# The output projection of a hybrid decoder layer by one level of Strassen's algorithm, with the weight sums made early and kept in DRAM

## The chip, the cores and the metric

One core of one Trainium2 chip. The metric is the time of one execution in device microseconds; lower is better. One execution was also recorded by the profiler, and the line numbers below are those of its kernel.

## The reference

The layer maps x of shape (1, 1024, 1024) to the same shape. Cut to what matters here:

```python
h = rmsnorm(x, g_pre) * (1 + scale) + shift        # scale, shift, gate from silu(c) @ w_mod
proj = h @ w_in                                    # split among three groups of heads
y_m = mlstm(...) * silu(mz)                        # 384 columns
y_a = sliding_window_attention(...) * silu(az)     # 384 columns
y_s = stickbreak_attention(...) * silu(sz)         # 256 columns
y = concat([y_m, y_a, y_s]) @ w_out                # (1024, 1024) @ (1024, 1024)
out = x + gate * rmsnorm(y, g_post)
```

The change is in the last product. All is float32.

## The kernel before, in words

Every large matmul is done in three passes: each float32 operand is split into a rounded high part and the low rest (`split`, L68 to L71: ScalarE or another engine casts, VectorE or GpSimd (POOL) subtracts), and TensorE adds high x high, high x low and low x high into one PSUM bank. `hh` and `hl` are the two parts of the transposed activations, eight k-tiles of 128 rows by 1024 tokens. They hold h for the projections, and later y for the output projection. All loads and stores go through `load` (L64) on SyncE's (SP's) queue, in order; a DMA that must wait holds back those behind it.

TensorE's order is written out by hand. Up to the first projections the order of the other engines is too; from there on a scheduler orders VectorE, ScalarE, POOL and SP, and each of them works strictly in the order that it chose.

The stages that the change and the steps below touch:

- The short convolution (L506 to L514) reads `mup`, the mLSTM's input, three slabs of 1027 columns, and makes `cu`; ScalarE's sigmoid of it is `cusg`. Meanwhile TensorE runs the projection `ptmif` (L385), whose banks ScalarE empties (v and igf, L446, L447).
- The gate chain (L562 to L618) computes the mLSTM's gates, max-stabilised running sums of 32 rows. It goes back and forth between TensorE (transposes into `gtr`) and VectorE and ScalarE (fx, ab, b_, a_, cm, mp, M_, em). Between its steps TensorE does pieces of other projections, given by a `Filler` (`fill`), so that it need not wait. Beside it the gate row is summed from `w_gate` (L529 to L540).
- The mLSTM loop (L640 to L749) runs over eight chunks of 128 tokens. Each loads `mbc` (a stabiliser, from DRAM), makes the decay matrix `e` (VectorE subtracts, POOL masks, ScalarE takes the exponential), and multiplies: qps, kps, sps, cps, nps on TensorE, with copies of qps (`q`, L674) on ScalarE and the masked scores `am` on VectorE between them.
- The gated projections: `gated` (L468 to L485) multiplies a branch's output with silu of its z. For y tiles 0 to 5 it splits the result and stores both parts in `d_yh`, `d_yl`; tiles 6 and 7 (from `ys`) are split into `hh`, `hl` near the end (`late`).
- The output projection (L1068 to L1138). `wo_load` loads and splits all of w_out into `woh` and `wol`, and `y_load(n)` brings half n of the tokens (512 columns) of y back into `hh`, `hl`. `out_mm(i, n, k)` does three matmuls for token block i (128 tokens), output half n (512 columns) and k-tile k. The first four blocks fill all eight PSUM banks, k outermost; the last four go one by one. `out_fin(i)` takes the sum of squares on ScalarE straight from PSUM, multiplies by the gate row `gbc`, raises the mean square to the power -1/2 on POOL, and adds x, loaded into `xr` (two buffers).

## Time and profile before

| what | value |
|---|---|
| three runs | 552.19, 553.53, 555.82 us; median 553.53 |
| the profiled execution | 553.0 us |
| its span, first to last instruction | 551.2 us |
| TensorE busy | 523.9 us in 2953 matmuls |
| mean granted TensorE clock | 0.997 of full speed |
| bytes moved by DMA | 96.57 MB |

The profile's rows name an engine (PE is TensorE, DVE VectorE, ACT ScalarE, POOL GpSimd, SPq SyncE's queue), a line, an operation and its tiles as out<-in. In a row of the order of time the first number is the start and the second the duration, both in microseconds; the bracket tells how long the engine had been idle before and what released it. A row by groups ends with busy time and the mean of one in ns. A row of a stretch has its limits and length, then busy time and count of PE, PE's weight loads, DVE, ACT and POOL, then granted clock, DMA share and GB/s. A DMA row ends with the median time from issue to landing. TensorE's matmuls overlap, so their pace is read from starts and counts, not from the duration of one.

### The profile page before, as it was taken

The page shows a single profiled execution, that of the slowest core. Times are in us where ns is not written, and L with a number is a line of the kernel's source. Part 1 is how long each engine was busy: PE and PEld are TensorE (multiplying, and loading weights), DVE is VectorE, ACT ScalarE, POOL GpSimd, SP SyncE. Part 2 cuts the span into 40 slices and gives each one's busy share as a digit, 9 for nine tenths or more (in the row PEclk, how much of TensorE's full clock was granted, in tenths as well). Part 3 has the DMA queues.
Part 4 walks back from the last instruction along what each step waited for, and adds up shares of the span by engine and source line. Part 5 has one row for each costly group of instructions (what it writes and reads, how often), then busy time and mean ns, then how long its engine had stood idle before and what let it go on. Part 6 is the DMA issues. An engine that isn't in the chain of part 4 may idle for free.

```text
span 551.2 us, 8550 instructions
## 1 busy us (share of the span) xinstructions
PE 523.9 (95%) x2953; PEld 449.0 (81%) x2953; DVE 332.5 (60%) x750; ACT 250.3 (45%) x571; POOL 220.6 (40%) x206
## 2 busy tenths in 40 slices
PE   4799999999998999999998999899999999999995
PEld 3577899899987989888786888788888888888884
DVE  4686692053707887678887479787878442108232
ACT  5643533451113333267677568667668432213100
POOL 2365765420033343234534348574766433111000
PEclk9999999999999999999999999999999999999998
DMA  8982360247986455699843389455421169607421
GB/s 307 417 293 75 120 227 21 59 145 219 284 240 222 135 162 125 162 268 299 238 150 98 125 226 249 142 149 167 134 77 59 39 193 404 238 5 238 144 84 69
DMA packets 63659, 96.57 MB, mean 175 GB/s; under 512 B 17600, under 2 KB 36992, under 8 KB 63488
## 3 DMA queue, kind: packets, MB, share of 16 engines
q1 hardware_dynamic: 63616, 96.03, 54.8%
q8 instruction: 23, 0.38, 0.3%
q14 instruction: 20, 0.16, 0.1%
HBM read 69.24 MB, written 25.20 MB: 171 GB/s over the span
## 4 chain that ended last, share of the span: by engine, by line
PE 78%; DVE 10%; DMA 4%; ACT 3%; issue 2%; POOL 2%; SPq 1%; DVEq 0%; POOLq 0%; ACTq 0%
PE pd L359 24%; PE ptav L385 6%; PE mu L233 6%; PE op L1109 5%; PE op L1108 5%; PE op L1107 5%; PE tp L994 3%; DMA ka<-d_akl 3%; PE ptmif L385 2%; DVE cu L509 2%; PE ops L1012 2%; PE ops L1013 2%; PE xps L166 2%; PE z L963 2%; PE mr L197 1%
## 5 line engine op out<-in xcount | busy, mean ns | idle before, releaser
L359 PE MATMUL pd<-hh,wl_d 128*128 128x512 f32 x256 | 71.1, 399 | 0.0
L359 PE MATMUL pd<-hh,wh_d 128*128 128x512 f32 x256 | 70.6, 400 | 0.0
L359 PE MATMUL pd<-hl,wh_d 128*128 128x512 f32 x256 | 70.6, 398 | 0.0
L302 POOL TENSOR_TENSOR wl_d<-w_d,wh_d 128x512 fp32r<-128x512 f32 x32 | 44.0, 1398 | 29.1 <-ACT wh_d L300 19.6
L359 PEld LDWEIGHTS pd<-hh,wh_d 128*128 128x128 f32 x256 | 46.1, 188 | 8.4 <-issue 0.5
L359 PEld LDWEIGHTS pd<-hl,wh_d 128*128 128x128 f32 x256 | 46.1, 188 | 8.0
L359 PEld LDWEIGHTS pd<-hh,wl_d 128*128 128x128 f32 x256 | 45.8, 188 | 7.7
L1108 PE MATMUL op<-woh,hl 128*128 128x512 f32 x128 | 50.6, 396 | 0.0
L1109 PE MATMUL op<-wol,hh 128*128 128x512 f32 x128 | 50.6, 396 | 0.0
L1107 PE MATMUL op<-woh,hh 128*128 128x512 f32 x128 | 50.6, 396 | 0.0
L982 POOL TENSOR_TENSOR sg<-sg,pr 128x512 f32<-128x512 f32 (+1 forms) x30 | 31.1, 1041 | 20.8 <-DVE pr L980 20.6
L857 POOL TENSOR_SCALAR zb<-zb,mx 128x256 f32<-128x256 f32 (+1 forms) x24 | 21.6, 914 | 42.5 <-DVE mx L854 28.4
L70 ACT CAST ah<-tp 128x512 fp32r<-128x512 f32 (+2 forms) x56 | 24.3, 436 | 29.2 <-PE tp L994 20.8
L71 DVE TENSOR_TENSOR al<-tp,ah 128x512 fp32r<-128x512 f32 (+2 forms) x56 | 27.4, 493 | 16.7 <-ACT ah L70 16.0
L1120 ACT ACTIVATE sj<-op 128x512 f32<-128x512 f32 x16 | 9.5, 597 | 50.4 <-PE op L1109 47.9
L1109 PEld LDWEIGHTS op<-wol,hh 128*128 128x128 f32 x128 | 24.0, 188 | 5.9
L1108 PEld LDWEIGHTS op<-woh,hl 128*128 128x128 f32 x128 | 24.0, 188 | 5.8
L1107 PEld LDWEIGHTS op<-woh,hh 128*128 128x128 f32 x128 | 24.0, 188 | 5.8
L1124 POOL TENSOR_TENSOR st<-st,mhalf 128x1 f32<-128x1 f32 x8 | 4.4, 554 | 57.5 <-DVE st L1123 57.5
L847 ACT ACTIVATE zb<-zb,mx 128x256 f32<-128x256 f32 (+1 forms) x48 | 23.2, 488 | 7.8 <-PE az L823 6.6
L980 DVE TENSOR_TENSOR_SCAN pr<-z,mzero 128x128 f32<-128x128 f32 (+3 forms) x32 | 25.6, 815 | 0.6 <-ACT z L971 0.2
L969 ACT ACTIVATE sg<-z 128x512 f32<-128x512 f32 (+3 forms) x48 | 23.8, 496 | 1.3 <-PE z L966 1.1
(247 smaller groups left out, 1328.4 us busy)
## 6 DMA issues: line engine op xcount, KB each, us to landing
wm<-in_w_ss_dram SPq DMA_DIRECT2D x16, 512.0 KB, 7.7
w_d<-in_w_dm_dram SPq DMA_DIRECT2D x16, 512.0 KB, 3.8
xt<-in_x_dram SPq DMA_DIRECT2D x8, 512.0 KB, 7.8
wg<-in_w_gate_dram SPq DMA_DIRECT2D x8, 512.0 KB, 5.8
wo<-in_w_out_dram SPq DMA_DIRECT2D x8, 512.0 KB, 5.2
xr<-in_x_dram SPq DMA_DIRECT2D x8, 512.0 KB, 4.7
out_dram<-ot SPq DMA_DIRECT2D x16, 256.0 KB, 2.3
hh<-d_yh SPq DMA_DIRECT2D x12, 256.0 KB, 6.0
```

The costliest lines, as they stand in the source:

```text
L70: e_hi(dst_h, src)
L71: e_lo.tensor_tensor(out=dst_l, in0=src, in1=dst_h.bitcast(F32), op=ALU.subtract)
L233: T.matmul(mu_acc[j][n], w[:, cs], h[:, k, t], start=(k == 0 and w is wh and h is hh), stop=(k == KT - 1 and h is hl))
L302: G.tensor_tensor(out=wl[:, a:b], in0=z[:, a:b], in1=wh.bitcast(F32)[:, a:b], op=ALU.subtract)
L359: T.matmul(ps, w[:, k, :], h[:, k, t], start=(k == 0 and w is wh and h is hh), stop=(k == KT - 1 and h is hl))
L385: T.matmul(ps[:, 0:self.N], h[:, k, t], w[:, k % 2, :], start=(k == 0 and q == 0), stop=(k == KT - 1 and q == 2))
L969: A.activation(sg[:, 0:w], zps[:, 0:w], AF.Sigmoid)
L980: V.tensor_tensor_scan(out=rev(pr), data0=rev(zps), data1=mzero[:, 0:1].to_broadcast([P, w]), initial=1.0 if nxt is None else nxt, op0=ALU ...
L982: (G if w > 256 and (h > 0 or i > 3) else V).tensor_tensor(out=sg[:, 0:w], in0=sg[:, 0:w], in1=pr[:, 1:w + 1], op=ALU.mult)
L1107: T.matmul(o, hh[:, k, t], woh[:, k, cs], start=(k == 0), stop=False)
L1108: T.matmul(o, hl[:, k, t], woh[:, k, cs], start=False, stop=False)
L1109: T.matmul(o, hh[:, k, t], wol[:, k, cs], start=False, stop=(k == KT - 1))
```

## The change

The 1024 x 1024 x 1024 product is cut into 2 x 2 blocks of 512. Instead of eight block products there are seven, of sums of blocks of y and of w_out (the variant with shared sums S1 to S4 and T1 to T4). With y in rows by token half i and columns by k half r, and w_out in rows by r and columns by output half n:

- P1 = y11 w11, P2 = y12 w21, P6 = S2 T2, P5 = S1 T1, P3 = S4 w22, P7 = S3 T3, P4 = y22 T4, in this order on TensorE. S1 = y21 + y22, S2 = S1 - y11, S4 = y12 - S2, S3 = y11 - y21.
- `w_sums` makes T1 to T4 from w_out, split into two parts, and stores them in DRAM (`d_th`, `d_tl`). For each of four c it loads two 512 KB pieces into the space of `mup`, makes four differences in place, and splits and stores each: 16 differences, 16 casts, 16 low parts, 8 loads and 32 stores of 256 KB. It is called in the gate chain, behind `tcol`.
- `gated` now also stores y unsplit in `d_y`, and for the second half of tokens it no longer splits and stores tiles 0 to 3.
- w11, w21 and w22 are loaded and split in the output stage (`w_ready`, twelve pieces of 256 KB), the T's are loaded there already split (`t_ready`, two loads of 1 MB each, into two pairs of buffers). `y_ready` makes the sums of y into `ysum`, four chunks c each, and splits them into `hh`, `hl` over blocks that are no longer needed.
- Each product has four groups of 12 matmuls, one per token block, into four banks; `e1` to `e7` empty them, adding to what earlier products left in SBUF (`u1`, `u3`, `o11`). Squares are taken from SBUF. `finish` does the rest of `out_fin`, for the first four blocks behind P3 and for the last four behind P4.

```diff
+    def w_sums():
+        for c in range(4):
+            z = mup.rearrange("p a b -> p (a b)")[:, 0:2 * D].rearrange("p (r a b) -> p r a b", r=2, a=2)
+            load(z[:, 0], w_out[c].rearrange("p (a b) -> p a b", a=2))
+            load(z[:, 1], w_out[4 + c].rearrange("p (a b) -> p a b", a=2))
+            w11, w12, w21, w22 = z[:, 0, 0, :], z[:, 0, 1, :], z[:, 1, 0, :], z[:, 1, 1, :]
+            for n, o, a, b in ((0, w11, w12, w11), (2, w12, w22, w12), (1, w22, w22, w11), (3, w21, w22, w21)):
+                V.tensor_tensor(out=o, in0=a, in1=b, op=ALU.subtract)
+                h = gp_.tile([P, 512], F32R, tag="th", bufs=2, name=f"th{c}{n}")
+                l = gp_.tile([P, 512], F32R, tag="tl", bufs=2, name=f"tl{c}{n}")
+                split(h, l, o, A.copy, V)
+                store(d_th[n, :, c, :], h)
+                store(d_tl[n, :, c, :], l)
...
+                store(d_y[dst_j, :, t], y)
+                if n == 1 and dst_j < 4:
+                    return
...
+    w_sums()
     mg_stk.close()
...
+    def y_ready(i, r, chunk):
+        for c in range(4):
+            k = 4 * r + c
+            split(hh[:, k, halves[i]], hl[:, k, halves[i]], chunk(c), A.copy, V)
...
+    w_ready("11", 0, 0)
     fill.through(I_SZ1)
     y_load(0)
+    w_ready("21", 1, 0)
     fill.through(99)
     y_load(1)
+    y_ready(1, 0, lambda c: summed(yc(c), y_quarter(1, 0, c), y_quarter(1, 1, c), ALU.add))
...
+    def product(yi, yr, w, evac):
+        wh, wl = wq_[w]
+        ps = [fbank(f"p{w}_{i}") if i == 3 else ops_.tile([P, 512], F32, tag="op", name=f"p{w}_{i}")
+              for i in range(4)]
+        for i in range(4):
+            t = slice(yi * 512 + i * P, yi * 512 + (i + 1) * P)
+            for c in range(4):
+                k = 4 * yr + c
+                T.matmul(ps[i], hh[:, k, t], wh[:, c, :], start=(c == 0), stop=False)
+                T.matmul(ps[i], hl[:, k, t], wh[:, c, :], start=False, stop=False)
+                T.matmul(ps[i], hh[:, k, t], wl[:, c, :], start=False, stop=(c == 3))
+            evac(i, ps[i])
...
+    def e2(i, ps):
+        V.tensor_tensor(out=o11[i], in0=ps, in1=u1[i], op=ALU.add)
+        square(o11[i], i, 0)
+        V.tensor_tensor(out=o11[i], in0=o11[i], in1=gbc[:, halves[0]], op=ALU.mult)
...
+    def e4(i, ps):
+        V.tensor_tensor(out=u1[i], in0=u1[i], in1=ps, op=ALU.subtract)
+        square(u1[i], 4 + i, 0)
+        finish(4 + i, ((0, u1[i], True), (1, u3[i], False)))
+
+    product(0, 0, "11", e1)
+    t_ready(2)
+    y_ready(0, 0, lambda c: summed(yc(c), yc(c), y_quarter(0, 0, c), ALU.subtract))
+    product(0, 1, "21", e2)
+    t_ready(1)
+    y_ready(0, 1, lambda c: summed(yc(c), y_quarter(0, 1, c), yc(c), ALU.subtract))
+    product(0, 0, "t2", e6)
+    w_ready("22", 1, 1)
...
+    y_ready(0, 0, s3)
+    product(1, 0, "t1", e5)
+    t_ready(3)
+    product(0, 1, "22", e3)
+    t_ready(4)
+    product(0, 0, "t3", e7)
+    product(1, 1, "t4", e4)
```

Since a scheduler sets the order of all engines but TensorE, three places show how their instructions now stand.

VectorE between P2 and P6. Before, the operations on this engine in the output stage were only the finishing of blocks (ot is a block's output, st its statistics):

```order
L71 TENSOR_TENSOR wol_5096<-wo7_5170,woh_5095 128x1024
L1122 TENSOR_TENSOR ot0_5413<-op0_0_5228,gbc_74 128x512
L1123 TENSOR_SCALAR st0_5412<-st0_5412 128x1
L1125 TENSOR_TENSOR ot0_5413<-op0_1_5232,gbc_74 128x512
L1122 TENSOR_TENSOR ot1_5435<-op1_0_5236,gbc_74 128x512
L1128 SCALAR_TENSOR_TENSOR ot0_5413<-ot0_5413,st0_5412,xr0_5410 128x512 x2
```

Now (p21_3 is P2's fourth bank, o113 the sum into which it is emptied; yo and three digits is a loaded chunk of y by i, r and c; ys holds y's tiles 6 and 7):

```order
L1201 TENSOR_TENSOR o113_5369<-p21_3_5454,u13_5361 128x512
L1203 TENSOR_TENSOR o113_5369<-o113_5369,gbc_74 128x512
L1131 TENSOR_TENSOR ysum_5206<-yo102_5339,ys_3612 128x512
L1131 TENSOR_TENSOR ysum_5206<-yo103_5344,ys_3612 128x512
L71 TENSOR_TENSOR hl_102<-ysum_5206,hh_101 128x512
L1131 TENSOR_TENSOR ysum_5206<-ysum_5206,yo000_5431 128x512
...
L1131 TENSOR_TENSOR ysum_5206<-ysum_5206,yo001_5436 128x512
L71 TENSOR_TENSOR hl_102<-ysum_5206,hh_101 128x512 x2
L1131 TENSOR_TENSOR ysum_5206<-ysum_5206,yo002_5441 128x512
L1131 TENSOR_TENSOR ysum_5206<-ysum_5206,yo003_5446 128x512
...
L1131 TENSOR_TENSOR ysum_5206<-yo010_5523,ysum_5206 128x512
```

Where rows are left out stands another low part of a chunk (hl), and one more stands behind the last row. The last two chunks of S1, all of S2 and the first chunk of S4 stand behind the emptying of P2's last bank.

ScalarE at the start of the mLSTM loop (wh_d is a weight cast, sh_aq_1 an eviction, q_0 the copy of qps for chunk 0, e the exponentials of chunks 0 and 1). Before:

```order
L300 CAST wh_d_1688<-w_d_1640 128x1024
L421 ACTIVATE sh_aq_1_1611<-pd_1_1586 128x512
L674 COPY q_0_1622<-qps_1617 96x512
L664 ACTIVATE e_1542<-e_1542 128x512
L664 ACTIVATE e_1634<-e_1634 128x512
L717 COPY num_1672<-nps_1667 128x388
```

Now:

```order
L688 ACTIVATE e_1665<-e_1665 128x512
L688 ACTIVATE e_1757<-e_1757 128x512
L303 CAST wh_d_1811<-w_d_1763 128x1024
L424 ACTIVATE sh_aq_1_1734<-pd_1_1709 128x512
L698 COPY q_0_1745<-qps_1740 96x512
L741 COPY num_1795<-nps_1790 128x388
```

The two exponentials moved ahead of the cast, the eviction and q_0.

VectorE around the start of the gate chain (fx and li are its first operations). Before, they came right behind the convolution:

```order
L509 SCALAR_TENSOR_TENSOR cu_799<-mup_103,col_62,cu_799 128x1024 x9
L587 MEMSET mp_1207 1x36
L569 TENSOR_SCALAR fx_1126<-gtr_1122,bi_1060 32x128
L573 TENSOR_SCALAR li_1125<-gtr_1122,bi_1060 32x128
L574 TENSOR_SCALAR fx_1126<-fx_1126 32x128
```

Now (th and tl are the two parts of a sum, by c and the number of T less one):

```order
L71 TENSOR_TENSOR tl11_1375<-mup_106,th11_1374 128x512
L71 TENSOR_TENSOR tl13_1382<-mup_106,th13_1381 128x512
L558 TENSOR_TENSOR mup_106<-mup_106 128x512
L71 TENSOR_TENSOR tl20_1391<-mup_106,th20_1390 128x512
L592 TENSOR_SCALAR fx_1129<-gtr_1125,bi_1063 32x128
L596 TENSOR_SCALAR li_1128<-gtr_1125,bi_1063 32x128
L597 TENSOR_SCALAR fx_1129<-fx_1129 32x128
L558 TENSOR_TENSOR mup_106<-mup_106 128x512
L425 SCALAR_TENSOR_TENSOR sl_ak0_0_1149<-pd7_0_1076,sh_ak0_0_1148 128x512
L598 TENSOR_TENSOR fx_1129<-fx_1129,ab_1133 32x128
```

The first two rounds of the sums and the first quarter of the third stand ahead of fx, and the rest stands between the operations of the chain.

More of the change, by code (lines that the diff above doesn't have):

```diff
@@ new lines, in rows_of, with square, finish @@
+    def rows_of(name):
+        return [op_.tile([P, 512], F32, tag=name, bufs=4, name=f"{name}{i}") for i in range(4)]
+    u1, u3, o11 = (rows_of(z) for z in ("u1", "u3", "o11"))
+    st = op_.tile([P, NT, 4], F32, name="st")
+    def square(src, i, n):
+        sj = op_.tile([P, 512], F32, tag="sj", bufs=2, name=f"sj{i}_{n}")
+        A.activation(sj, src, AF.Square, accum_out=st[:, i, n:n + 1])
+    def finish(i, parts):
+        xr = op_.tile([P, D], F32, tag="xr", bufs=2, name=f"xr{i}")
+        load(xr, x[i * P:(i + 1) * P, :])
+        s_ = st[:, i, :]
+        V.tensor_scalar(out=s_[:, 2:3], in0=s_[:, 1:2], scalar1=s_[:, 0:1], scalar2=D * EPS, op0=ALU.add, op1=ALU.add)
+        G.tensor_tensor(out=s_[:, 3:4], in0=s_[:, 2:3], in1=mhalf[:, 0:1], op=ALU.pow)
+        for n, o, gate in parts:
+            if gate:
+                V.tensor_tensor(out=o, in0=o, in1=gbc[:, halves[n]], op=ALU.mult)
+        for n, o, _ in parts:
+            V.scalar_tensor_tensor(out=o, in0=o, scalar=s_[:, 3:4], in1=xr[:, halves[n]], op0=ALU.mult, op1=ALU.add)
+            store(out[i * P:(i + 1) * P, halves[n]], o)
@@ new lines, in e7 @@
+    def e7(i, ps):
+        V.tensor_tensor(out=u1[i], in0=ps, in1=u1[i], op=ALU.add)
+        V.tensor_tensor(out=u3[i], in0=ps, in1=u3[i], op=ALU.add)
+        square(u3[i], 4 + i, 1)
+        V.tensor_tensor(out=u3[i], in0=u3[i], in1=gbc[:, halves[1]], op=ALU.mult)
+    def e4(i, ps):
[4 more added lines that the diff above has]
+    t_ready(2)
@@ new lines, in trunk, with s3 @@
+    y_ready(0, 0, lambda c: summed(yc(c), yc(c), y_quarter(0, 0, c), ALU.subtract))
[4 more added lines that the diff above has]
+    w_ready("22", 1, 1)
+    def s3(c):
+        z = y_quarter(0, 0, c)
+        return summed(z, z, y_quarter(1, 0, c), ALU.subtract)
+    y_ready(0, 0, s3)
[4 more added lines that the diff above has]
+    product(0, 0, "t3", e7)
```

93 lines of the change are left out of this document (42 added, 51 removed).

## The prediction

> **What bounds the kernel now.** I read the page's first and fourth parts, then busy time by stretches, then single stretches in order of time.
>
> ```profile
> span 551.2 us, 8550 instructions
> PE 523.9 (95%) x2953; PEld 449.0 (81%) x2953; DVE 332.5 (60%) x750; ACT 250.3 (45%) x571; POOL 220.6 (40%) x206
> PE 78%; DVE 10%; DMA 4%; ACT 3%; issue 2%; POOL 2%; SPq 1%; DVEq 0%; POOLq 0%; ACTq 0%
> ```
>
> TensorE is busy for 95% of the span and is 78% of the chain that ended last, so a microsecond of its work removed is worth a microsecond, unless it waits instead. The stretches show where it has no waits:
>
> ```profile
> 455.20:545.00 89.80, 89.76 (x385) 71.95 (x383) 27.98 (x43) 18.13 (x39) 12.62 (x12) 1.00 0.48 173
> 150.00:170.00 20.00, 17.47 (x90) 14.05 (x89) 6.63 (x11) 3.83 (x6) 7.92 (x7) 1.00 0.80 237
> ```
>
> The output projection is 455.2 to 545.0: 384 matmuls in 89.8 us, 0.2338 us each, with no gap; VectorE is busy for only 28.0 us of it. At 150 to 170, where the mLSTM loop starts, TensorE already idles 2.5 us.
>
> **What is removed.** Seven products of 4 x 4 x 3 = 48 matmuls are 336 instead of 384: 48 x 0.2338 = **-11.2 us**. Nothing else leaves the path.
>
> **What is added in the output stage.** The prices of its operations:
>
> ```profile
> L1120 ACT ACTIVATE sj<-op 128x512 f32<-128x512 f32 x16 | 9.5, 597 | 50.4 <-PE op L1109 47.9 <-DVE st L1123 1.5 <-DVE ot L1128 1.0
> L1122 DVE TENSOR_TENSOR ot<-op,gbc 128x512 f32<-128x512 f32 x8 | 5.5, 691 | 20.4 <-ACT sj L1120 20.1 <-DMA out_dram<-ot 0.2
> L1128 DVE SCALAR_TENSOR_TENSOR ot<-ot,st,xr 128x512 f32<-128x512 f32 x16 | 11.3, 748 | 1.8 <-DMA xr<-in_x_dram 1.2
> L1124 POOL TENSOR_TENSOR st<-st,mhalf 128x1 f32<-128x1 f32 x8 | 4.4, 554 | 57.5 <-DVE st L1123 57.5
> 456.13 1.29 DVE L71 TENSOR_TENSOR hl<-ys,hh 128x512 fp32r<-128x512 f32 x2 [1.83 <-ACT hh L70]
> 459.43 0.62 ACT L70 CAST hh<-ys 128x512 fp32r<-128x512 f32 x1 [2.83 <-POOL ys L484]
> ```
>
> A 128x512 operation takes VectorE 0.69 us, 0.645 in a row of two; a cast takes ScalarE 0.62.
>
> The products follow each other as P1, P2, P6, P5, P3, P7, P4. P1 and P2 need what the old code also had there (y of the first half, unsummed, and w_out), so from 455.2 on P1 ends at 466.4 and P2 at 477.6 (11.2 each). P6 needs the row sum S2 = S1 - y11, four chunks, each a VectorE subtraction, a ScalarE cast and a VectorE subtraction for the low part. VectorE works in order, and in its order two of S1's chunks and all of S2 stand **behind P2's fourth eviction**, although P2 reads none of them. That eviction cannot start before P2's last matmul is done, at 477.8. So: the eviction 0.69, ScalarE's square of it 0.60, the gating multiply that waits for the square 0.68, together 2.0, to 479.8; then to the low part of S2's fourth chunk 13 operations (six sums, six low parts and S4's first sum, which stands between) x 0.645 = 8.4, with the casts beside them, to 488.3; then P6's last two matmuls of its first group, to 488.8. Without the wait this group would end at 477.6 + 2.8 = 480.4. **+8.4 us**: TensorE idles until S2's first chunk at about 483, and then crawls. Bounds: 8.0 if every hand-over is hidden, 10.5 if S2's last two y loads, which are issued behind t1's two loads of 1 MB, land late. These are 2.1 MB from 477.7 on, at the rate of slice 34 of the page's row (404 GB/s) 5.2 us:
>
> ```profile
> GB/s 307 417 293 75 120 227 21 59 145 219 284 240 222 135 162 125 162 268 299 238 150 98 125 226 249 142 149 167 134 77 59 39 193 404 238 5 238 144 84 69
> xr<-in_x_dram SPq DMA_DIRECT2D x8, 512.0 KB, 4.7
> out_dram<-ot SPq DMA_DIRECT2D x16, 256.0 KB, 2.3
> ```
>
> so they end near 483, and the y chunks behind them are there when VectorE comes to them at 485. By the same rate t2 (from 466.5), t3 (from 508.5) and t4 (from about 520 to 528) are in before P6, P7 and P4 (530.8); P5, P3 and P7 find their sums and weights ready, because nothing but P2's evictions stood ahead of them. Their cover is 2 to 6 us; if t4 were later than that, P4 would wait for the difference.
>
> **The end.** Before, it is this:
>
> ```profile
> 544.56 0.40 PE L1109 MATMUL op<-wol,hh 128*128 128x512 f32 x1
> 546.72 1.42 DVE L1128 SCALAR_TENSOR_TENSOR ot<-ot,st,xr 128x512 f32<-128x512 f32 x2
> 547.50 0.99 SPq L64 DMA_DIRECT2D out_dram<-ot  x2
> ```
>
> From the last matmul (544.96) to the end are 6.2 us, 3.1 of them behind the last VectorE operation (548.1). Now each row block is finished in 2.8 us instead of 5.6, and it has two buffers for the x rows: block 7's x load is issued behind block 5's two stores. With P4 ending at 455.2 + 78.4 + 8.4 = 542.0, block 5's stores are issued until about 542.3, x lands 4.7 us later at 547.0, then two operations (1.4) and 3.1: 551.4, 9.4 us behind the last matmul. **+3.2 us**; at least 1.4 (if x were there, VectorE's own chain of subtract, square, gate and two multiplies would end at 546.6), at most 4.
>
> **The start of the mLSTM loop** is not edited, but its ScalarE and POOL order came out another way: q_0's copy now stands behind both decay exponentials, a weight cast and an eviction.
>
> ```profile
> 160.51 0.94 SPq L64 DMA_DIRECT2D mbc<-d_m  x2
> 164.97 1.00 DVE L661 TENSOR_TENSOR e<-tcol,mbc 128x512 f32<-128x512 f32 x1 [7.35 <-DMA mbc<-d_m]
> 161.74 1.05 ACT L300 CAST wh_d<-w_d 128x1024 fp32r<-128x1024 f32 x1 [4.84 <-PE pd L359]
> 163.18 0.57 ACT L674 COPY q<-qps 96x512 f32<-96x512 f32 x1
> 166.62 1.68 POOL L662 TENSOR_SCALAR_AFFINE_SELECT e<-e 128x512 f32<-128x512 f32 x2
> 167.75 1.22 ACT L664 ACTIVATE e<-e 128x512 f32<-128x512 f32 x2 [3.99 <-POOL e L662]
> 163.91 1.06 PE L690 MATMUL sps<-q,cuh 96*128 96x128 f32 x8
> 169.59 1.13 PE L712 MATMUL nps<-v,am 128*128 128x97 f32 x8 [1.00 <-DVE am L692]
> ```
>
> Before, q_0 was there at 163.75 and the exponentials (from 167.75) held up only am. Now mbc is issued ahead of two stores, 1.2 us sooner; e follows 4.5 us behind, at 163.8; the second e ends near 165.7, its mask 166.5, its exponential 167.1, the cast 168.1, the eviction 168.6, q_0 169.1. sps starts at 169.1 instead of 163.9, the old waits behind it vanish, and nps follows after sps, cps and five fillers (2.6 us as before), near 171.7: **+2.0 us** (0 if mbc lands 2 us sooner, +3 if later).
>
> **The sums of w_out** stand in VectorE's and SP's queues ahead of and between the gate chain.
>
> ```profile
> 82.99 1.06 ACT L513 ACTIVATE cusg<-cu 128x1024 f32<-128x1024 f32 x1 [2.74 <-DVE cu L509]
> 87.64 1.06 ACT L513 ACTIVATE cusg<-cu 128x1024 f32<-128x1024 f32 x1 [2.33 <-POOL cu L514]
> 89.18 0.45 PE L385 MATMUL ptmif<-wh_mif,hh 128*128 128x392 f32 x1 [0.93 <-ACT igf L447]
> 107.93 0.34 DVE L569 TENSOR_SCALAR fx<-gtr,bi 32x128 f32<-32x128 f32 x1 [17.86 <-POOL wl_av L302]
> 113.58 0.28 DVE L575 TENSOR_TENSOR fx<-fx,ab 32x128 f32<-32x128 f32 x1 [0.93 <-ACT ab L572]
> 114.65 0.41 DVE L579 TENSOR_TENSOR_SCAN cm<-ones,a__1128 32x128 f32<-32x128 f32 x1
> 116.29 0.12 PE gtr L582
> w_d<-in_w_dm_dram SPq DMA_DIRECT2D x3, 512.0 KB, 3.2
> d_akh<-sh_ak SPq DMA_DIRECT2D x2, 256.0 KB, 2.0
> ```
>
> VectorE idles 17.9 us ahead of fx, and the new work fills that. The convolution has read the first slab of mup at 83.0, so the first half block lands at 86.2, is subtracted by 86.9 and cast by 87.5, just ahead of the third cusg (87.64), behind which TensorE already waits 0.9 us for igf. A round of one c is a load 3.2, then subtraction, cast, low part (1.9), one store (2.4 with its issue) for the two buffers, cast and low part (1.3): about 9 us. Two rounds end near 103 and the first quarter of the third near 106, ahead of fx at 107.9. Between fx and cm stand five more operations, 3.2 us; VectorE waited 0.9 there, cm had 1.2 us to spare before the transpose at 116.29, and ScalarE's table loads come earlier, since a weight cast moved behind them. I take **+0.5 us**, bounds 0 and 6 (below).
>
> **Clock.** Where TensorE idles, the granted clock falls:
>
> ```profile
> 547.00:548.00 1.00, 0.00 (x0) 0.00 (x0) 1.00 (x2) 0.00 (x0) 0.00 (x0) 1.00 0.00 0
> 548.00:549.00 1.00, 0.00 (x0) 0.00 (x0) 0.13 (x1) 0.00 (x0) 0.00 (x0) 0.70 0.65 248
> 549.00:550.00 1.00, 0.00 (x0) 0.00 (x0) 0.00 (x0) 0.00 (x0) 0.00 (x0) 0.50 0.71 277
> ```
>
> 0.70 in one microsecond means half from 548.4 on, 3.4 us behind the last matmul. The two new waits are each about 5 us. The trace never shows it come back. Behind the wait at P6 twelve matmuls crawl at VectorE's pace for 5.6 us, which even half speed (0.47 each) keeps, so the clock may be back by then: **+0.7 us**, bounds 0 and 8.4 (P6's other 36 matmuls all at half speed).
>
> By the Trainium skill, TensorE: Matmul & The Clock Gate, section "HAM oscillation — how this bites in real kernels", gaps beyond about 3.4 us throttle TensorE to half until it has been busy again for a window as long; with that figure each wait costs an estimated 1.7 us more and the sum would be 2.7 us higher. The fall at 548.4 agrees with it; no run here shows the return.
>
> **Sum:** -11.2 + 8.4 + 3.2 + 2.0 + 0.5 + 0.7 = +3.6 us: span 554.8. The profiled execution took 553.0 for its span of 551.2, so 556.6; the median of the runs shown is 553.5, half a microsecond above it: **557.0 us**.
>
> **Rivals.**
>
> *The clock stays down* (slower). One mechanism at one place: P6. If TensorE is not back at full speed at 488.8, its 36 remaining matmuls cost 0.47 each, +8.4 instead of +0.7: 564.7. It decides once the idle time is past 3.4 us; for it, the rows above; against it, the twelve matmuls between. The Trainium skill's rule above lies between this and my sum.
>
> *The sums are late in the gate chain* (slower). If loads land as w_out's own did in the output stage,
>
> ```profile
> wo<-in_w_out_dram SPq DMA_DIRECT2D x8, 512.0 KB, 5.2
> ```
>
> each round is 2.0 longer: 2.25 rounds before fx are 4.5 late against 2 to spare, and 1.75 rounds inside the chain another 3.5. Then +6: 562.5. It decides if fx starts after 108. Against it: the DMA row of 3.2 is from this very stretch.
>
> *The saving comes through* (faster). If VectorE's rest had S2 ready at 477.6 and q_0 were not late, -11.2 + 3.2 + 0.5 = -7.5: 546. For it: 62 us of VectorE's 90 are idle there. Against it: its order, which no early data can change, since the eviction ahead waits for P2 itself.
>
> **How the numbers follow.** My case has 0.65, the clock 0.14, the late sums 0.13, the saving 0.08. 1%, 5.5 us, is about what a measurement of this kernel can tell from no change: 548.0 to 559.1. My case's own range is 551 to 562; 0.54 of it lies within 1% and 0.11 above. Faster 0.08, same 0.54, slower 0.11 + 0.14 + 0.13 = 0.38. The range 550.5 to 564.5 leaves out the saving and the worst of the two slow cases.
>
> **What would show it.** Right: 48 fewer matmuls; one TensorE wait of 5 to 6 us between P2 and P6, released by VectorE's or ScalarE's S2, with granted clock below 1 behind it; P6's first group 8 us long; last matmul to end 8 to 10 us, with VectorE waiting for x; sps waiting for q_0. Wrong: P6 starting within 2 us of P2's end, or fx later than 108.5.

## The result, and the profile after

The change makes the kernel slower: 576.62 us (median of four, 574.58 to 577.86) against 553.62 for the kernel before on the same chip, a ratio of 1.0414 with a 95% interval of 1.0385 to 1.0444. The forecast was 557.0, in a range of 550.5 to 564.5. The profiled execution took 577.86. Its page begins, and names the chain that ended last, so:

```profile
span 576.0 us, 8758 instructions
PE 526.3 (91%) x2905; PEld 448.8 (78%) x2905; DVE 395.7 (69%) x850; ACT 267.5 (46%) x607; POOL 212.0 (37%) x198
PE 61%; DVE 16%; DMA 12%; ACT 4%; SPq 3%; issue 3%; POOL 1%; DVEq 0%; ACTq 0%
```

The 48 matmuls are gone, yet TensorE is busy 2.4 us longer than before: part of what is left ran at a lower clock. VectorE and the DMAs now hold 28% of the chain where they held 14%. To find the place, put the start of the same instruction beside itself in both traces (us from the start of the span):

| instruction | before | after | later by |
|---|---|---|---|
| gtr of igf, first of the gate chain | 107.5 | 113.1 | 5.6 |
| gtr of cm | 116.2 | 129.7 | 13.5 |
| carry | 127.4 | 143.6 | 16.2 |
| gbps, the gate row | 148.9 | 166.8 | 17.9 |
| first nps of the mLSTM loop | 169.6 | 189.9 | 20.3 |
| first matmul of the output projection | 455.2 | 476.2 | 21.0 |
| end of the span | 551.2 | 576.0 | 24.8 |

So 20 us are lost between 84 and 190 us, none to speak of in the two attention loops, and the output stage gives 3.8 more where it should have given back 11.2.

**The gate chain.** TensorE's waits from 80 to 172 us in the trace after (total, times, longest); before, up to the start of gbps, it waited 0.9 us for igf and for nothing else:

```profile
PE ptmif L388 <- ACT igf L450: 4.3, 2, 2.3
PE ptav L388 <- DVE sl_ak L425: 3.7, 1, 3.7
PE gtr L605 <- DVE cm L602: 2.0, 1, 2.0
PE gbps L571 <- DVE gacc L545: 1.5, 1, 1.5
```

These are 11.5 us. The rest is nearly all the clock, an estimated 6.9 us (TensorE's busy time at half clock up to gbps, halved). By the busy time in stretches, 124 to 134 us is, first before, then after,

```profile
124.00:134.00 10.00, 10.00 (x60) 9.71 (x59) 2.60 (x6) 0.96 (x2) 0.00 (x0) 1.00 0.75 181
```

```profile
124.00:134.00 10.00, 8.04 (x27) 7.46 (x27) 9.14 (x19) 4.66 (x9) 6.56 (x4) 0.50 0.90 271
```

27 matmuls instead of 60, at half the granted clock (0.50), behind the wait for sl_ak and around the one for cm. The first wait, for igf, is read from VectorE, ScalarE and GpSimd in order of time:

```profile
84.51 9.01 POOL L520 TENSOR_TENSOR cu<-cu,cusg 128x1024 f32<-128x1024 f32 x3 [4.65 <-ACT cusg L519]
86.88 1.65 DVE L558 TENSOR_TENSOR mup<-mup 128x512 f32<-128x512 f32 x1 [1.15 <-DMA mup<-in_w_out_dram]
88.61 0.62 ACT L70 CAST th<-mup 128x512 fp32r<-128x512 f32 x1 [2.92 <-DVE mup L558]
89.13 1.05 ACT L519 ACTIVATE cusg<-cu 128x1024 f32<-128x1024 f32 x1
91.21 3.59 DVE L558 TENSOR_TENSOR mup<-mup 128x512 f32<-128x512 f32 x2
94.11 0.62 ACT L70 CAST th<-mup 128x512 fp32r<-128x512 f32 x1 [3.49 <-DVE mup L558]
```

ScalarE's casts of the sums (th) wait 2.9 and 3.5 us for VectorE's subtractions, which beside GpSimd's gating of cu take 1.65 and 1.8 us each where they take 0.68 alone (95.37 us in the same trace); the third cusg starts at 89.13 instead of 87.64, and the copies of igf stand behind. Then fx, on VectorE:

```profile
112.14 1.54 DVE L71 TENSOR_TENSOR tl<-mup,th 128x512 fp32r<-128x512 f32 x1 [1.83 <-DMA d_tl<-tl]
117.17 0.69 DVE L71 TENSOR_TENSOR tl<-mup,th 128x512 fp32r<-128x512 f32 x1 [2.88 <-DMA d_tl<-tl]
117.78 0.33 DVE L592 TENSOR_SCALAR fx<-gtr,bi 32x128 f32<-32x128 f32 x1
```

Its transpose was there at 113.4. fx started 4.4 us later, behind a low part of the sums that waited for a store to free its buffer.

**The output stage.** TensorE ends P2 and begins P6:

```profile
498.36 0.40 PE L1170 MATMUL p<-wql,hh 128*128 128x512 f32 x1
504.31 0.80 PE L1168 MATMUL pt<-wqht,hh 128*128 128x512 f32 x1 [5.56 <-ACT hh L70]
509.60 0.79 PE L1168 MATMUL pt<-wqht,hh 128*128 128x512 f32 x1 [1.63 <-ACT hh L70]
512.63 0.63 PE L1168 MATMUL pt<-wqht,hh 128*128 128x512 f32 x1
514.73 0.40 PE L1170 MATMUL pt<-wqlt,hh 128*128 128x512 f32 x1
```

and VectorE, meanwhile, has the order that the forecast named, with one wait more:

```profile
498.79 0.69 DVE L1201 TENSOR_TENSOR o<-p,u 128x512 f32<-128x512 f32 x1 [0.57 <-PE p L1170]
500.33 0.69 DVE L1203 TENSOR_TENSOR o<-o,gbc 128x512 f32<-128x512 f32 x1 [0.85 <-ACT sj L1181]
500.94 1.29 DVE L1131 TENSOR_TENSOR ysum<-yo,ys 128x512 f32<-128x512 f32 x2
508.21 1.44 DVE L1131 TENSOR_TENSOR ysum<-ysum,yo 128x512 f32<-128x512 f32 x2 [2.02 <-DMA yo<-d_y]
```

The second group of P6 starts at 512.63; without a wait it would have started at 501.4 (498.6 and 12 matmuls of 0.2333), so 11.2 us are lost there and about 1.2 more by the half clock, which lasts to 514.7: the matmuls stand 0.43 apart until then. In sum: first to last matmul 476.19 to 567.04 is 90.85 us, of which 336 x 0.2333 = 78.4 are work and 12.4 are lost; the tail behind the last matmul is 9.0 where it was 6.2. And 78.4 - 89.8 + 12.4 + 2.8 = +3.8, the stage's part of the loss.

### The profile page after: what moved, and what is told of

The parts are those of the page before. It is cut to its first block, busy times and chain, and to the rows that moved or that the text cites. A ratio compares the mean times of both kernels' runs of the same rounds, so it can differ in the third digit from the quotient of the medians.

```text
span 576.0 us, 8758 instructions
## 1 busy us (share of the span) xinstructions
PE 526.3 (91%) x2905; PEld 448.8 (78%) x2905; DVE 395.7 (69%) x850; ACT 267.5 (46%) x607; POOL 212.0 (37%) x198
## 4 chain that ended last, share of the span: by engine, by line
PE 61%; DVE 16%; DMA 12%; ACT 4%; SPq 3%; issue 3%; POOL 1%; DVEq 0%; ACTq 0%
PE pd L362 21%; PE mu L236 6%; PE ptav L388 4%; SPq L64 3%; PE tp L1018 3%; DVE cu L515 2%; PE xps L169 2%; PE ops L1036 2%; PE ops L1037 2%; DMA mup<-in_w_out_dram 2%; PE p L1170 1%; PE p L1168 1%; PE p L1169 1%; PE z L987 1%; DMA out_dram<-o 1%
## 5 line engine op out<-in xcount | busy, mean ns | idle before, releaser
L1189 POOL TENSOR_TENSOR st<-st,mhalf 128x1 f32<-128x1 f32 x8 | 7.5, 932 | 84.6 <-DVE st L1188 84.6
L1168 PE MATMUL pt<-wqht,hh 128*128 128x512 f32 x64 | 27.0, 423 | 7.2 <-ACT hh L70 7.2
L388 PE MATMUL ptav<-wh_av,hh 128*128 128x384 f32 x64 | 24.0, 375 | 3.7 <-DVE sl_ak L425 3.7
L1169 PE MATMUL pt<-wqht,hl 128*128 128x512 f32 x64 | 27.0, 422 | 0.4 <-DVE hl L71 0.4
L388 PE MATMUL ptmif<-wh_mif,hh 128*128 128x392 f32 x64 | 22.7, 355 | 4.3 <-ACT igf L450 4.3
L1170 PE MATMUL pt<-wqlt,hh 128*128 128x512 f32 x64 | 26.6, 415 | 0.0
L995 ACT ACTIVATE z<-z 128x512 f32<-128x512 f32 (+3 forms) x48 | 24.0, 501 | 0.0
L388 PE MATMUL ptav<-wh_av,hl 128*128 128x384 f32 x64 | 23.4, 366 | 0.0
```

Source lines behind the costliest of these rows:

```text
L388: T.matmul(ps[:, 0:self.N], h[:, k, t], w[:, k % 2, :], start=(k == 0 and q == 0), stop=(k == KT - 1 and q == 2))
L995: A.activation(zps[:, 0:w], zps[:, 0:w], AF.Sigmoid, scale=-1.0)
L1168: T.matmul(ps[i], hh[:, k, t], wh[:, c, :], start=(c == 0), stop=False)
L1169: T.matmul(ps[i], hl[:, k, t], wh[:, c, :], start=False, stop=False)
L1170: T.matmul(ps[i], hh[:, k, t], wl[:, c, :], start=False, stop=(c == 3))
```

## The experiments

The theory after the result: the sums of w_out cost about 18 to 20 us where they stand, and the output stage nets +4 because P6 waits for S2. Rival: the loss is made in the output stage and its loads. All ratios below are to the kernel before on the same chip.

### Which part costs what

*sums_alone*: the kernel before with `w_sums` as in the change.

```diff
+    d_th, d_tl = dram("d_th", [4, P, 4, 512]), dram("d_tl", [4, P, 4, 512])
+    def w_sums(): ...
     acol, wscol, emcol = tcol[:, 0:32], tcol[:, 32:64], tcol[:, 64:96]
+    w_sums()
```

> The kernel before, with the sums of w_out made and kept in DRAM at the same place of the program as in the change, and never read; the output projection is the old one. Theory (the sums cost most of the loss, in the gate chain, where the start of the gbps matmuls moved from 148.9 to 166.8 us): 553.6 + 18 = 571.6 us, between 568 and 575, with gbps at 165 to 168 us. Rival (the sums are hidden and the loss is made in the output stage and by the loads of the loop): within 1% of the kernel before, 551 to 558 us.

574.21 us, ratio 1.0369 (1.0330 to 1.0407): +20.4. The start of gbps is 166.7, the start of the output projection 474.4, 19.2 late.

*no_sums*:

```diff
-    w_sums()
...
-        load(h, d_th[n - 1])
-        load(l, d_tl[n - 1])
+        for dst, src in ((h, d_qh), (l, d_ql)):
+            load(dst, src.rearrange("c (p t) (u b) -> (c p) (t u) b", t=2, u=2))
```

> The changed kernel without the sums: the pairs t1 to t4 are loaded from two other arrays in DRAM of the same size, so these four products multiply the wrong weights; every load, product and sum of the output stage stays. Theory: the loss of the gate chain (17.9 us at gbps) goes and the rest stays, 576.6 - 18 = 558.6 us, between 556 and 561: still over the kernel before by the mLSTM start (+2.4) and the output stage (+3.8, measured from the last pd matmul to the end). Rival (the loss comes from the output stage): over 570 us. Second rival (with the sums gone the output stage pays too, as the prediction's rival of the full saving): 546 us.

557.3 us, 1.0067 (1.0042 to 1.0091): +3.5. Its output projection starts at 455.0 as before and takes 100.1 us (before 96.0). The two parts add up: 20.4 + 3.5 = 23.9, the change 23.0. The rival has fallen: five sixths of the loss are the sums.

*sums_no_stores*: sums_alone without

```diff
-                store(d_th[n, :, c, :], h)
-                store(d_tl[n, :, c, :], l)
```

> As sums_alone, with the 32 stores of the rounded sums and remainders left out: the loads of w_out and all work of VectorE and ScalarE stay, nothing is kept. If the wait is for buffers that stores free and for a queue that is full of transfers: 553.6 + 0 to 6, that is 554 to 560 us. If the order and the length of the VectorE and ScalarE instructions set it: 567 to 573 us, nearly what sums_alone takes. Between them, 560 to 567 us, both have a share, and the difference to sums_alone is the share of the stores.

565.27 us, 1.0215 (1.0171 to 1.0259): +11.5, between the two. The stores have a share of 8.9. Next the rest was cut the other way.

*engines_only*: sums_no_stores without the two loads.

> As sums_no_stores, with the loads of w_out left out as well: the 16 subtractions, 16 casts and 16 remainders run at the same place on what the buffer of the convolution holds, nothing is loaded or kept. sums_no_stores took 565.3 us, 11.6 over before. If VectorE, with its fixed order, mostly waits there for the loads to land (7.9 us of its waits in sums_no_stores are on them) and the gate chain stands behind: 554 to 559 us. If the instructions themselves cost it, by their number, their order ahead of the gate chain's and their length beside GpSimd (subtractions of 1.5 to 2 us where 0.69 is the least): 560 to 566 us.

561.19 us, 1.0146 (1.0131 to 1.0161): +8.1. This is in the range of the second theory, the instructions themselves. gtr of igf is at 114.6, 7.1 late, and carry, gbps and nps are 8.4 to 8.5 late. How much of this is the order and how much the subtractions' greater length beside GpSimd is not separated. ScalarE's row and TensorE's, in order of time:

```profile
94.69 0.62 ACT L70 CAST th<-mup 128x512 fp32r<-128x512 f32 x1 [4.19 <-DVE mup L552]
```

```profile
98.28 0.69 PE L387 MATMUL ptmif<-wh_mif,hh 128*128 128x392 f32 x1 [3.70 <-ACT igf L449]
```

*moves_only*: the sums' 8 loads and 32 stores, with w_out stored as it is.

```diff
-                V.tensor_tensor(out=o, in0=a, in1=b, op=ALU.subtract)
...
-                split(h, l, o, A.copy, V)
-                store(d_th[n, :, c, :], h)
-                store(d_tl[n, :, c, :], l)
+                store(d_th[n, :, c, :], o)
+                store(d_tl[n, :, c, :], o)
```

> The kernel before with the transfers of the sums alone: w_out is loaded into the same buffer (4 MB) and stored twice to DRAM (8 MB) as it is, with no subtraction, cast or remainder. sums_no_stores and sums_alone differ by 8.9 us. If that is the transfers in the queue ahead of the loads of w_av and w_gate: 558 to 563 us, most of it after the carry, where gbps waits for the gate row. If the stores cost only through buffers for which VectorE and ScalarE wait: 553 to 556 us.

565.54 us, 1.0236 (1.0193 to 1.0279): +12.5, more than expected. Its gtr of igf is on time (107.6), then carry is 6.7 late, gbps 7.9, the first nps 11.2. ScalarE's waits name the cause:

```profile
ACT wh_av L302 <- DMA w_av<-in_w_av_dram: 10.1, 2, 6.8
```

(4.4 us before): the loads of w_av stand in SP's queue among 4 MB in and 8 MB out; the second of the last two is issued at 109.79 where both were out by 104.2 before, since the queue stood from 104.3 to 108.1 ahead of a load of w_out into space that a store had to leave first. The same happens to w_gate. So the loss is two prices that add: 8.1 for the instructions and 12.5 for the transfers are 20.6, and sums_alone had 20.4. They add in the whole, not at each mark: carry is 8.4 and 6.7 late in the two and 13.1 in sums_alone.

*engines_v*: engines_only with the casts moved from ScalarE to VectorE, to see whether ScalarE's order carries the 8.1.

```diff
-                split(h, l, o, A.copy, V)
+                split(h, l, o, V.tensor_copy, V)
```

> engines_only with the 16 casts on VectorE instead of ScalarE; still nothing loaded or kept. In engines_only the copy of igf out of PSUM stands on ScalarE behind a cast of the sums that waits 4.2 us for VectorE (whose subtractions last 1.4 to 1.7 us beside GpSimd), and TensorE waits 5.2 us for that copy; gtr of igf starts 7.1 us later than before. Theory (ScalarE's order carries the engines' share of 8.1 us): with the casts away from it, gtr of igf starts at 107 to 109 us and the time is 553.5 to 556.5 us. Rival (VectorE's own order, with the gate chain's fx, b and a behind the sums, and now 16 more instructions on it): 559 to 564 us.

566.24 us, 1.0265 (1.0204 to 1.0326): a miss in the time and a hit in the place. gtr of igf is at 108.5, within the 107 to 109 of the theory; but now the gate chain waits on the other engine, since VectorE is busy without a pause from 94 to 122 us and fx, which is in its order behind the sums, starts at 122.0. Neither engine's order alone is the cause: whichever has the sums ahead of the chain holds it up.

### The output stage

*yo_early*: the change with ten buffers for the loaded parts of y and their loads for S1 and S2 ahead.

```diff
-        z = wop.tile([P, 512], F32, tag="yo", bufs=4, name=f"yo{i}{r}{c}")
+        z = wop.tile([P, 512], F32, tag="yo", bufs=10, name=f"yo{i}{r}{c}")
...
-    y_ready(1, 0, lambda c: summed(yc(c), y_quarter(1, 0, c), y_quarter(1, 1, c), ALU.add))
+    y1 = [(y_quarter(1, 0, c), y_quarter(1, 1, c)) for c in range(4)]
+    y0 = [y_quarter(0, 0, c) for c in range(4)]
+    y_ready(1, 0, lambda c: summed(yc(c), *y1[c], ALU.add))
...
-    y_ready(0, 0, lambda c: summed(yc(c), yc(c), y_quarter(0, 0, c), ALU.subtract))
+    y_ready(0, 0, lambda c: summed(yc(c), yc(c), y0[c], ALU.subtract))
```

> The changed kernel with ten buffers instead of four for the loaded parts of y, and the ten loads for S1 and S2 issued one after the other before S1; nothing else. VectorE's order then has the pieces of S2 between the evictions of P2. Theory (P6 waits for S2, first matmul at 504.3 after a P2 that ends at 498.8, second group at 512.6 where 501.4 would be without a wait, 11.2 us of it by the wait and the half clock that follows): 576.6 - 8 to 11, that is 565.5 to 568.5 us, with the granted clock at 1.00 through P6. Rival (P6 is held by the t2 load or by weights, not by S2; or the clock falls there anyway): 574 to 577 us.

571.48 us, 1.0313 (1.0266 to 1.0360): -5.1 against the change, less than expected. The stage takes 94.5 us instead of 99.8 in the recorded execution (567.66 us, the fastest of the four; it is also 4.8 us ahead where the stage begins, behind code that is the same). With the data there earlier the scheduler put S2 between P2's evictions, and TensorE's waits in the stage became

```profile
PE pt L1170 <- DMA wqht<-d_th: 2.7, 1, 2.7
PE pt L1172 <- DMA wqlt<-d_tl: 1.7, 1, 1.7
```

The t2 load stood behind two loads of rows of x. So the stage was fed further, on top of no_sums.

*no_sums_fed*: no_sums with yo_early, and

```diff
-        wq_[name] = [wop.tile([P, 4, 512], F32R, tag=z, bufs=2, name=f"{z}{name}") for z in ("wqh", "wql")]
+        wq_[name] = [wop.tile([P, 4, 512], F32R, tag=z, bufs=3, name=f"{z}{name}") for z in ("wqh", "wql")]
...
+    with tc.high_priority(offset=3000):
+        t_ready(2)
     product(0, 0, "11", e1)
-    t_ready(2)
```

> no_sums (the pairs t1 to t4 are loaded from other arrays of the same size, so four products multiply the wrong weights) with the buffers of yo_early, a third pair of weights, and the t2 load issued ahead of P1. In yo_early the output stage took 94.5 us instead of 99.8, and P6 still waited 4.4 us, now for the t2 load behind the rows of x. Theory (the stage loses its saving to P6's wait, the half clock behind it and the tail): P6 starts when P2 ends, the stage takes 88 to 91 us, and the time is 545 to 549 us, faster than before. Rival (another bound stands behind it, the transfers that fill the queue from 455 to 506 us or VectorE's evictions): 551 to 556 us.

553.30 us, 1.0003 (0.9980 to 1.0026): the rival. P6 lost 7.2 us again, now to parts of y that came late, while the DMA share was 1.03 and more from 455 to 485 us:

```profile
465.00:475.00 10.00, 10.00 (x45) 8.04 (x44) 6.62 (x11) 3.77 (x8) 0.00 (x0) 1.00 1.03 406
475.00:485.00 10.00, 5.91 (x20) 3.86 (x19) 9.15 (x16) 6.39 (x13) 0.00 (x0) 0.89 1.03 410
```

*no_sums_early*: no_sums_fed with 1.75 MB of that loaded earlier. At step 30 of the last attention's loop `ahead()` is called, which loads w11 and y21's first three chunks into buffers of their own; the first uses take them from there. Also

```diff
-        xr = op_.tile([P, D], F32, tag="xr", bufs=2, name=f"xr{i}")
+        xr = op_.tile([P, D], F32, tag="xr", bufs=3, name=f"xr{i}")
```

> no_sums_fed (four products multiply the wrong weights) with 1.75 MB of its loads (w11 and three parts of y) taken ahead in the loop of the last attention, and three buffers instead of two for the rows of x. There the queue moves 400 GB/s without a pause from 455 to 485 us, S1 and S2 wait for parts of y, and P6 still loses 7.2 us; the tail after the last matmul is 9.5 us where it was 6.2. Theory (the transfers of the first 30 us of the stage are what P6 waits for): P6 loses 0 to 3 us, the stage takes 89 to 92 us, the time is 547 to 550.5 us. Rival (VectorE, busy 19 of 20 us from 475 to 495, is the bound): P6 loses 5 us or more, 552 to 554 us.

543.21 us, 0.9824 (0.9803 to 0.9846): faster than before by 9.7 us, and under what the theory had. TensorE goes from P2 into P6 without a pause:

```profile
478.33 0.40 PE L1188 MATMUL p<-wql,hh 128*128 128x512 f32 x1
478.56 0.40 PE L1186 MATMUL pt<-wqht,hh 128*128 128x512 f32 x1
```

The stage takes 86.1 us: 78.57 from the first to the last matmul, 7.6 behind it. The saving of seven products is thus real and whole (-11.2), in a kernel that does not make the sums of w_out, at the price of a tail 1.3 longer. What had eaten it was the transfers ahead of P6: of the 9.0 us by which the recorded stages of no_sums_fed and no_sums_early differ, 7.1 are lost matmul time and 1.9 the tail. That VectorE was the bound, the other theory, has fallen for this kernel.

### A cheaper place for the sums

In these five the sums of w_out are made again, now in the loop of the last attention, kept unrounded (4 MB out instead of 8), and split in the output stage.

*raw_in_loop*: the output stage of no_sums_fed, and

```diff
+    def w_sum(c):
+        z = kp.tile([P, 2, 2, 512], F32, tag="wz", bufs=1, name=f"wz{c}")
+        load(z[:, 0], w_out[c].rearrange("p (a b) -> p a b", a=2))
+        load(z[:, 1], w_out[4 + c].rearrange("p (a b) -> p a b", a=2))
...
+            V.tensor_tensor(out=o, in0=a, in1=b, op=ALU.subtract)
+            store(d_t[n, :, c, :], o)
...
+        if s in (8, 16, 24, 32):
+            w_sum((8, 16, 24, 32).index(s))
```

> The same output stage as no_sums_fed, with the right weights: the sums of w_out are made in four pieces in the loop of the last attention, kept in DRAM unrounded (4 MB instead of 8) and split in the output stage as the other weights are. Added: 16 subtractions of 0.69 us in a loop where VectorE is idle 28 of 105 us, 16 casts and 16 remainders of 0.6 to 0.7 us in the output stage, where VectorE is idle some 25 of 90. Theory (the place of the sums cost the 20 us, not the sums): 546 to 551 us, not slower than before. Rival (the sums cost what they cost wherever VectorE runs in order): 556 us or more.

564.33 us, 1.0201 (1.0185 to 1.0216): the rival, +11.0 over no_sums_fed. From the first ops to the output projection it takes 128.8 us instead of 118.2. TensorE's waits there:

```profile
PE z L979 <- DVE pr L996: 7.3, 4, 3.3
```

(0.4 in no_sums_fed). In this trace 3.7 us more lie ahead of 110 us, where the code is the same (3.3 of them ahead of 20 us, by the first matmul of mu); they are not explained.

*raw_late*: raw_in_loop with the pieces called at steps 27, 30, 33 and 36, y21's three chunks loaded ahead, and three buffers for x.

> raw_in_loop with its four pieces of sums about 13 steps later in the loop of the last attention, three parts of y loaded ahead, and three buffers for the rows of x. raw_in_loop lost 10.6 us in that loop, where the matmuls of z waited 7.3 us for VectorE's products while its subtractions ran from 339 to 396 us (VectorE 8.2 of 10 busy there without them, 6.9 from 400 to 440). Theory (the loss follows from how full VectorE is where the sums stand): the loop loses 3 to 6 us, 556 to 560 us. Rival (each of the 16 subtractions delays a chain of the loop wherever it stands): 562 to 566 us.

555.20 us, 1.0045 (1.0027 to 1.0063). Better than expected, though not for the reason given: the scheduler still placed the subtractions from 336 to 397 us, and the loop still lost 8.9 us; the stage fell from 93.6 to 90.8 and the unexplained 3.7 us were not there.

*raw_later*: raw_late with the first load tied to the third head's output.

```diff
+        if c == 0:
+            for r in range(2):
+                V.tensor_copy(z[0:64, r, 0, 0:1], ys[0:64, 1, 0:1])
```

> raw_late with one more dependence: the first load of the sums waits for the output of the third of the four heads (a copy of one column, 406 us in the trace of raw_late), so that the 16 subtractions stand behind 400 us in VectorE's order, where it has 2.3 of 10 us free up to 430 and 5.5 of 10 behind that. In raw_late they still ran from 336 to 397 us, and the output stage began at 464.7 us, 8.5 us after that of no_sums_early. Theory (a chain pays for the sums only where the engine has no room beside it): the loop loses 2 to 5 us instead of 8.5 and the time is 549 to 552.5 us, up to the kernel before or a little under it. Rival (the sums displace the loop's chains there too, or the last stores hold up the loads of w11 behind them in the queue): 554 to 558 us.

554.14 us, 1.0027 (1.0010 to 1.0044). The loop loses 4.8 us as expected (2 to 5), with the 16 subtractions from 410 to 449 us; but the stage takes 92.1, and so the time is the rival's. It lost 6.1 us at P6, with VectorE full:

```profile
480.00:490.00 10.00, 7.29 (x27) 4.93 (x26) 10.00 (x17) 5.95 (x13) 0.00 (x0) 0.93 0.90 314
490.00:500.00 10.00, 10.00 (x40) 8.00 (x39) 10.00 (x18) 4.54 (x9) 0.00 (x0) 0.90 0.60 173
```

*x_rows_late* and *x_gate_late* ask whether that is the queue or VectorE. The first ties the first three loads of rows of x to P5's eviction; the second also moves four products with the gate row behind the norm.

```diff
+        if i < 3:
+            V.tensor_copy(xr[:, 0:1], u3[i][:, 0:1])
         load(xr, x[i * P:(i + 1) * P, :])
```

```diff
     def e2(i, ps):
         V.tensor_tensor(out=o11[i], in0=ps, in1=u1[i], op=ALU.add)
         square(o11[i], i, 0)
-        V.tensor_tensor(out=o11[i], in0=o11[i], in1=gbc[:, halves[0]], op=ALU.mult)
...
+                V.scalar_tensor_tensor(out=o, in0=o, scalar=s_[:, 3:4], in1=gbc[:, halves[n]], op0=ALU.mult, op1=ALU.mult)
+                V.tensor_tensor(out=o, in0=o, in1=xr[:, halves[n]], op=ALU.add)
```

> raw_later with the first three loads of rows of x tied to the eviction of P5 (a copy of one column), so that they no longer stand in the queue ahead of the parts of t2. In raw_later the output stage took 92.1 us against 86.1 in no_sums_early; from its first to its last matmul it lost 6.1 us, at P6. Theory A (the t2 parts land late behind 1.5 MB of x, 3.9 us at 400 GB/s): the loss falls by 3 to 4 us, time 550 to 551.5 us. Theory B (VectorE is full, 10 of 10 us from 480 to 500, and the remainders of t2 stand in its order between other work): it stays, 553 to 555 us.

> x_rows_late with the four products of output rows and gate that VectorE makes between P2's evictions (4 of 0.69 us) moved behind the norm, where they join its scaling. Theory A (the queue): the same time as x_rows_late within 1 us. Theory B (VectorE's room between 475 and 500 us): 2 to 3 us under x_rows_late. Both theories together: under 550 us, faster than before.

x_rows_late: 553.81 us, 1.0011 (0.9992 to 1.0030), the same as raw_later within its interval. P6's loss fell from 6.1 to 4.5 us and the wait moved from t2's remainders to S2's:

```profile
PE pt L1187 <- DVE hl L71: 1.7, 1, 1.7
```

but the rows of x now came late at the end (tail 9.3 instead of 7.6). x_gate_late: 550.97 us, 0.9950 (0.9928 to 0.9972), 2.8 under x_rows_late. The time is the one that theory B named, so with the sums made VectorE's room is likely the larger bound at P6 and the queue the smaller. Where in the stage the 2.8 us were won is not shown, since the granted clock in x_gate_late's trace is 0.85. It is the one version with sums of w_out that beats both kernels, by half a percent of before and 25 us of the change.

## Why the prediction was wrong, point by point

**What failed: "The sums of w_out", +0.5 us with bounds 0 and 6.** They cost 20.4 (sums_alone), and no bound of the forecast held that. fx started at 117.8, past the 108.5 that the forecast itself named as a sign of being wrong. Three things in the step were wrong.

- *It asked one question, whether fx would be late.* The loss starts before fx and goes on behind it. Before: ScalarE's casts stand between the convolution's sigmoids and the copies of igf, and wait there for VectorE (+5.6 at gtr of igf; engines_only +7.1). Behind: w_av and w_gate are loaded through the queue that carries the sums (moves_only: on time at igf, 11.2 late at nps). The step priced VectorE's room, and neither ScalarE's order nor SP's queue.
- *The durations were those of a quiet stretch.* It took 0.645 us for a subtraction, 3.2 for a load, 2.0 for a store. In the trace after these are, by groups,

```profile
L558 DVE TENSOR_TENSOR mup<-mup 128x512 f32<-128x512 f32 x16 | 14.1, 879 | 5.7 <-DMA mup<-in_w_out_dram 5.7
L71 DVE TENSOR_TENSOR tl<-mup,th 128x512 fp32r<-128x512 f32 x16 | 14.2, 887 | 10.5 <-DMA d_tl<-tl 7.4 <-ACT th L70 3.1
mup<-in_w_out_dram SPq DMA_DIRECT2D x8, 512.0 KB, 4.9
d_th<-th SPq DMA_DIRECT2D x16, 256.0 KB, 4.5
```

   0.88 us on the mean, and longer loads and stores in a queue that the sums fill. A round took some 13 us and not 9.
- *The lost time was counted without the clock*, which was at 0.50 from 91.4 to 94.8 us and from 122.1 to 135.8 us.

The rival "the sums are late in the gate chain" had the right sign and the right test, "if fx starts after 108" (117.8), but its price, +6, came from loads alone.

**S2 behind P2's last eviction, +8.4 (8.0 to 10.5), and the clock, +0.7.** The mechanism was right in every row: order, evictions, sums, crawl. The size is 11.2 + 1.2 = 12.4. The 2.8 us between 8.4 and 11.2 are the y loads, 2.0 late (the upper bound had them), 0.2 in P2's eviction chain and 0.6 in the last matmuls of P6's first group, which ran at half clock. One sentence beside it was wrong: that VectorE's order is one "which no early data can change". In yo_early, with ten buffers and the loads issued ahead, the scheduler chose another order.

**The clock.** At P6 the half clock ended at 514.7, so the rival "the clock stays down" (all of P6) did not happen. But the term priced the clock at P6 alone. Behind the shorter waits of the gate chain it cost the 6.9 us above, and at the start of the mLSTM loop (186.99 to 190.40) about 1.7. Nor does it take idle time past 3.4 us, as that rival had it: the first spell of half clock, at 91.4, follows a wait of 2.04 us. P6 in the stretches of the trace after, with the granted clock third from the right:

```profile
500.00:502.00 2.00, 0.00 (x0) 0.00 (x0) 1.67 (x3) 0.64 (x3) 0.00 (x0) 0.75 1.08 404
502.00:504.00 2.00, 0.00 (x0) 0.00 (x0) 1.92 (x4) 1.25 (x3) 0.00 (x0) 0.50 1.00 418
512.00:514.00 2.00, 2.00 (x6) 1.54 (x6) 2.00 (x5) 1.84 (x3) 0.00 (x0) 0.50 0.66 213
514.00:516.00 2.00, 2.00 (x9) 1.63 (x8) 2.00 (x4) 0.00 (x0) 0.00 (x0) 0.83 0.29 100
```

**The start of the mLSTM loop, +2.0.** Measured +2.4 between gbps and nps, with the wait that was named:

```profile
PE sps L714 <- ACT q L698: 3.6, 1, 3.6
```

It belongs to the sums: with their stores (sums_alone 1.0 us of this wait, moves_only 4.2) the exponentials stand ahead of q_0, and without them (no_sums, sums_no_stores, engines_only) the old order and no such wait are back. It is inside the 20.4. The near hit in size is in part luck: TensorE's waits between the two marks grew only by 1.1 us (2.5 to 3.6), and 1.5 is the half clock behind them, which the term did not have. In yo_early, with the same order, the distance grew by 0.4.

**The products, -11.2, and the tail, +3.2.** Both right: 336 matmuls instead of 384, whole in no_sums_early; the tail is +2.8, with VectorE's last operations waiting for x (0.84 us) as forecast.

Sum by the runs: -11.2 + 12.4 + 2.8 + 20.4 = +24.4; the spans differ by 24.8, the medians by 23.0.

## What to carry to other kernels

Work that no one waits for is not free when it goes into in-order queues ahead of a chain that someone does wait for: price it on every queue that it enters, the engine that casts, the DMA queue and its stores as well as the engine that has the room, and by durations beside what else runs there. Two experiments split such a loss well, the instructions without the transfers and the transfers without the instructions; here they added up in the whole. And a saving on TensorE comes through only as far as the next product is fed: here 1.75 MB loaded earlier, with a third buffer for the rows of x, was worth 10 us.

## What the runs showed of the hardware

VectorE's operations on SBUF lengthened while GpSimd worked on SBUF too: in engines_v a 128x512 subtraction took 0.68 us alone and 2.85 beside GpSimd, and a cast 0.41 and 2.43:

```profile
86.54 2.43 DVE L70 CAST th<-mup 128x512 fp32r<-128x512 f32 x1
88.89 2.85 DVE L552 TENSOR_TENSOR mup<-mup 128x512 f32<-128x512 f32 x1
94.47 0.41 DVE L70 CAST th<-mup 128x512 fp32r<-128x512 f32 x1
94.80 0.68 DVE L552 TENSOR_TENSOR mup<-mup 128x512 f32<-128x512 f32 x1
```

GpSimd's own three operations went from 8.15 us together before to 9.38 there. By the Trainium skill, SBUF — State Buffer, section "Who interferes with whom", a VectorE instruction with two SBUF inputs contends with a GpSimd instruction that reads SBUF, and so do casts in a two-port mode, one of the two engines blocking the other. The rows agree, and give the price: up to four times for the subtraction and six for the cast.

The granted clock moves on a grid. In the trace after it changes at 91.42, 94.83, 122.14, 135.79, 186.99, 190.40, 501.02, 514.67 and 569.28 us, read from stretches of 0.05 us. The distances between these times are whole multiples of 3.4133 us, within 0.02, and the changes in twelve other traces of these experiments lie on grids of the same step. What a wait costs thus depends on how it lies in the steps (TensorE's busy time is of 3.41 us):

| step of the trace after | TensorE busy, us | clock in it | clock in the next |
|---|---|---|---|
| 88.00 to 91.42, with the wait of 2.04 us | 1.38 | 1.00 | 0.50 |
| 91.42 to 94.83 | 3.41 | 0.50 | 1.00 |
| 98.24 to 101.65, start of the wait of 2.30 us | 2.81 | 1.00 | 1.00 |
| 101.65 to 105.07, rest of that wait | 1.72 | 1.00 | 1.00 |
| 118.72 to 122.13, start of the wait for sl_ak | 1.07 | 1.00 | 0.50 |
| 128.96 to 132.37, with the wait for cm | 2.70 | 0.50 | 0.50 |
| 132.37 to 135.79 | 3.41 | 0.50 | 1.00 |

A wait of 2.04 us within one step halved the clock, and a longer one that two steps shared did not. The clock came back behind the first step in which matmuls ran throughout, so half speed lasted one step in the first spell and four (13.65 us) behind the wait for sl_ak and at P6. Where the limit lies is open: in engines_only a step with 1.81 us of busy time was followed by a fall. By the Trainium skill, TensorE: Matmul & The Clock Gate, section "What's actually happening", the activity is watched in a window of about 3.4 us that runs freely, so where a change comes depends on where in the window the work lies. The trace agrees: the step is that window.
